# A blocked output projection with seven products in place of eight, behind an attention layer on one core

## The chip, the core and the metric

The kernel runs on one core of a Trainium2 chip. The metric is device time in microseconds of one execution. The core has a matrix engine (PE, with its weight loads as PEld), a vector engine (DVE), a scalar engine (ACT), a general engine (POOL) and a queue that issues transfers (SP); each runs its instructions in order and they wait for each other through semaphores.

## The reference

One post-norm layer over 1024 positions of width 1024. The input is normalised and modulated, one projection gives queries, keys, values and gates of 16 heads (8 forgetting heads, 8 stick-breaking heads of width 64), each head attends causally, the gated head outputs are concatenated to y, and the part that is changed here follows:

```python
y = jnp.concatenate([y_fox, y_sb], axis=-1) @ w_out[layer]
resid = DEEPNORM_ALPHA * x.astype(jnp.float32) + gate[:, None, :].astype(jnp.float32) * y.astype(jnp.float32)
x = _layer_norm(resid, ln_g[layer], ln_b[layer]).astype(dtype)
```

All is in float32. `w_out` is 1024 x 1024, `gate` is one row of 1024 numbers, the same for all positions.

## The kernel before

A product is computed from operands split in a high and a low part (`hi`, `lo`, type fp32r): three matmuls, high x high, low x high and high x low, take the place of one. The split costs a rounding copy for `hi` and a subtraction for `lo`.

The heads are handled in 8 pairs p = 0 to 7, of 128 rows each. A pair has 16 units (head h, query tile i of 128 positions), 128 units in all. A unit's scores come first, its transposition two units later (`LAG = 2`), and when both tiles of a 256-wide block are there `att_pv(p, h, j)` multiplies with v, and the 64 x 256 result is gated into `ty`. Between the units PE runs "fillers", generators that compute the in-projection of the pairs to come, one step per `yield`; a list of targets says how many steps run before each unit. The order of PE's instructions and the issue of the units is that of the Python code (`manual_schedule`); the other engines are ordered by a scheduler that follows the dependences. The last pair runs its tiles in falling order, so tiles 6 and 7 of y are finished first.

The output weights are prepared in the attention. `gen_split_out` (L812) runs beside the fillers of pairs 4 to 7: for each of 8 blocks of 128 rows and 2 halves of 512 columns, `fetch_w` loads a piece, POOL multiplies it by `gate` (L124), makes `hi` (L126) and `lo` (L127), and two transfers put them in `wo_dr` in memory; five filler steps lie between pieces (`SPACE = 5`). They come back by `load_wo` during the last fillers, into the buffers of the modulated input u, which is no longer needed then.

The outputs y of pairs 0 to 6 are stored to `y_dr` and loaded by tile with `load_y` (L832), where POOL makes `hi` and `lo` (L839, L840); y of pair 7 stays in SBUF (`y7h`, `y7l`, L520 to L525). The generator `tail` computes the output projection, some steps after each of the last units (`TAIL`) and the rest when the units are done, tile by tile in `OUT_ORDER = (6, 7, 4, 5, 2, 3, 0, 1)`. A step is `o_step(t, h, pr)`: three matmuls of 512 columns (L859 to L861). After 8 steps `o_half` adds ALPHA times x (L878, DVE) and takes the half's statistics on DVE (`bn_stats`, L879); after the second half come `bn_aggr` (L187), on POOL two steps on 128 x 1 (L189 adds epsilon, L190 takes the power -1/2), and on DVE two steps per half: L886 centres and multiplies by ln_g, L890 scales and adds ln_b; then the transfer out. The last tile's second half is cut in 320 and 192 columns, so that little is left after the last matmul.

Two accumulators in PSUM (`acc_tile`, a ring of two banks) serve the projection in turn: `o_6_0`, `o_6_1`, `o_7_0` and so on.

Of the kernel before, what the change touches and what calls it, by code (L numbers as in the profile page):

```python
# [27 lines left out]
def tile_hybrid_layer(  # L28
# [51 lines left out]
    SPACE = 5  # L80
# [29 lines left out]
    y_dr = dr.tile([NPAIR, P, SEQ], F32, tag="y_dr", name="y_dr")  # L110
    wo_dr = dr.tile([2, NPAIR, P, D], F32, tag="wo_dr", name="wo_dr")
# [256 lines left out]
    def gen_forget():  # L368
# [14 lines left out]
        for _ in range(FROW):  # L383
# [3 lines left out]
        nc.gpsimd.memset(tri, 1.0)  # L387
        nc.gpsimd.affine_select(out=tri, in_=tri, pattern=[[1, P]], base=0,
                                channel_multiplier=-1, compare_op=ALU.is_ge, fill=0.0)
# [43 lines left out]
    def att_scores(u, following):  # L433
# [28 lines left out]
        else:  # L462
# [14 lines left out]
            nc.gpsimd.tensor_tensor(be[:, :ke - 1], be[:, :ke - 1], kp[:, 1:ke], op=ALU.mult)  # L477
# [23 lines left out]
    y_last = []  # L501

    def att_pv(p, h, j):
# [298 lines left out]

    wo = {}

    def load_wo(pr):
        hi = big(f"u{pr}", 1, f"woh_{pr}", F32R)
        lo = big(f"v{pr}", 1, f"wol_{pr}", F32R)
        nc.sync.dma_start(hi.bitcast(F32), wo_dr[0, pr])
        nc.sync.dma_start(lo.bitcast(F32), wo_dr[1, pr])
        wo[pr] = (hi, lo)  # L810

    def gen_split_out():  # L812
        for pr in range(NPAIR):
            for h in range(2):
                s = slice(h * 512, h * 512 + 512)
                with after(*scaled[BEHIND:BEHIND + 1]):
                    hi, lo = fetch_w(f"o{pr}_{h}", w_out[pr * P:(pr + 1) * P, s], 512, gate[:, s])
                nc.sync.dma_start(wo_dr[0, pr, :, s], hi.bitcast(F32)[:, :512])
                nc.sync.dma_start(wo_dr[1, pr, :, s], lo.bitcast(F32)[:, :512])
                for _ in range(SPACE):  # L820
                    yield
# [8 lines left out]
    y_t = {}  # L830

    def load_y(t):  # L832
        ts_ = slice(t * P, (t + 1) * P)
        for p0, n in ((0, 4), (4, 3)):
            raw = raw_tile(f"yr_{t}_{p0}")[:, :n * P]
            nc.sync.dma_start(raw.rearrange("p (a q) -> p a q", q=P),
                              y_dr[p0:p0 + n, :, ts_].rearrange("a p q -> p a q"))
            hi, lo = y_t[t, p0 // 4] = ring_w(f"y_{t}_{p0}")
            nc.gpsimd.tensor_scalar(hi[:, :n * P], raw, 1.0, 1.0, op0=ALU.mult, op1=ALU.mult)  # L839
            nc.gpsimd.tensor_tensor(lo[:, :n * P], raw, hi.bitcast(F32)[:, :n * P], op=ALU.subtract)  # L840

    o_acc = {}
    OUT_ORDER = (6, 7, 4, 5, 2, 3, 0, 1)

    def groups(t):
        return ((0, 512), (512, 832), (832, 1024)) if t == OUT_ORDER[-1] else ((0, 512), (512, 1024))

    def o_step(t, h, pr):
        if pr == 0:
            o_acc[t, h] = (t_tile if h == 2 else acc_tile)(f"o_{t}_{h}")  # L850
        acc = o_acc[t, h]
        if pr == NPAIR - 1:
            yh, yl = (v[:, t * P:(t + 1) * P] for v in y_last)
        else:
            yh, yl = (v[:, pr % 4 * P:][:, :P] for v in y_t[t, pr // 4])
        hi, lo = wo[pr]
        s = slice(*groups(t)[h])
        acc = acc[:, :s.stop - s.start]
        nc.tensor.matmul(acc, yh, hi[:, s], start=(pr == 0), stop=False)  # L859
        nc.tensor.matmul(acc, yl, hi[:, s], start=False, stop=False)  # L860
        nc.tensor.matmul(acc, yh, lo[:, s], start=False, stop=(pr == NPAIR - 1))  # L861

    res = {}

    def o_half(t, h):
        ts_ = slice(t * P, (t + 1) * P)
        s = slice(*groups(t)[h])
        ng = len(groups(t))
        if h == 0:
            xr = big("k", 4, f"xr_{t}")  # L870
            nc.sync.dma_start(xr, x[ts_, :])
            res[t] = (att_tile(f"r_{t}"), xr, sb.tile([P, 3, 6], F32, tag="st", bufs=3, name=f"st_b{t}")[:, :ng, :])
        r, xr, st = res[t]
        last = t == OUT_ORDER[-1]

        acc = o_acc[t, h][:, :s.stop - s.start]
        to = acc if last else r[:, s]
        nc.vector.scalar_tensor_tensor(to, xr[:, s], ALPHA, acc, op0=ALU.mult, op1=ALU.add)  # L878
        nc.vector.bn_stats(st[:, h, :], to)  # L879
        if h == ng - 1:  # L880
            mv, rs = ln_finish(st, f"b{t}")
            cuts = [slice(*g) for g in groups(t)]
            mid = [o_acc[t, j][:, :c.stop - c.start] if last else r[:, c] for j, c in enumerate(cuts)]

            def first(j):
                nc.vector.scalar_tensor_tensor(mid[j], mid[j], mv[:, 0:1], lgb[0][:, 0, cuts[j]],  # L886
                                               op0=ALU.subtract, op1=ALU.mult)

            def second(j):
                nc.vector.scalar_tensor_tensor(r[:, cuts[j]], mid[j], rs[:, 0:1], lgb[0][:, 1, cuts[j]],  # L890
                                               op0=ALU.mult, op1=ALU.add)
                nc.sync.dma_start(out[ts_, cuts[j]], r[:, cuts[j]])

            if not last:
                for j in range(2):
                    first(j)
                    second(j)
                return
            for j in (1, 0, 2):
                first(j)  # L900
            c = cuts[1]
            nc.scalar.activation(r[:, c], mid[1], AF.Copy, scale=rs[:, 0:1])
            nc.gpsimd.tensor_tensor(r[:, c], r[:, c], lgb[0][:, 1, c], op=ALU.add)
            nc.sync.dma_start(out[ts_, c], r[:, c])
            for j in (0, 2):
                second(j)

    def gen_out_first(t):
        for h in range(2):
            for pr in range(NPAIR - 1):  # L910
                o_step(t, h, pr)
                yield

    def gen_out_last(t):
        for h in range(2):
            o_step(t, h, NPAIR - 1)
            o_half(t, h)
            yield

    def gen_out(t):  # L920
        for h in range(len(groups(t))):
            for pr in range(NPAIR):
                o_step(t, h, pr)
                if pr == NPAIR - 1:
                    o_half(t, h)
                yield


    def gen_last_g(p):
        tiles = fetch_m(p, 2)  # L930
        yield
# [64 lines left out]
    for k in range(len(units) + LAG + 1):  # L996
# [31 lines left out]
        if k == LAST:  # L1028
            load_y(6)
            load_ln()  # L1030
# [67 lines left out]
```

## Time and profile before

| | |
|---|---|
| median of 3 runs | 695.15 us (695.07 to 695.25) |
| the profiled execution | 695.03 us, span 693.3 us |
| granted clock of PE | 0.998 |
| busy: PE, DVE, POOL, ACT | 98%, 67%, 58%, 55% |
| transfers | 81.59 MB, mean 118 GB/s |

The page gives each engine's busy time as a share of the span, the chain of work that ended last, and groups of instructions; a group's row has the line, the engine, the operation, out <- in with shapes, the count, the busy time in us and the mean in ns of one, and then the idle time in front of them with what ended it. A row of the timeline has start and length in us. A row of stretches has, after the stretch and its length, busy us (and instruction count) of each engine, the granted clock, the DMA share and GB/s.

### The profile page before, as it was taken

Reading aid. Unit: us, or ns where it says so; the run is one execution under the profiler, and the core shown is the slowest. Engines: PE = TensorE matmul, PEld = TensorE weight load, DVE = VectorE, ACT = ScalarE, POOL = GpSimd, SP = SyncE. Lnnn points to the kernel's source line nnn. Section 1 sums busy time; section 2 is a strip of 40 time slices with the busy share of each in tenths; the row PEclk is TensorE's granted clock in tenths of the full one; section 3 lists DMA queues with packets and bytes.
Section 4 is the critical chain, followed back from the end, with each engine's and each line's share of the span. In section 5 each row is a group of like instructions: output and inputs, shape, how many; then the busy total and the mean of one; then the engine's idle time right before and its main releaser. Section 6 shows DMA issues by size and latency. Waiting matters only on the chain.

```text
span 693.3 us, 11762 instructions
## 1 busy us (share of the span) xinstructions
PE 678.1 (98%) x4031; PEld 592.2 (85%) x4031; DVE 465.9 (67%) x943; ACT 381.1 (55%) x857; POOL 399.1 (58%) x522
## 2 busy tenths in 40 slices
PE   8899999999999999999999999999999999999995
PEld 4689898888998888889998888889988889888885
DVE  6886868867658676767575665656665767774645
ACT  5566467756658666666674564655565666531000
POOL 5360086746438565556368787787685364655411
PEclk9999999999999999999999999999999999999999
DMA  9954531011102122112033554354352289143301
GB/s 328 415 205 160 168 104 47 25 40 45 47 9 69 41 54 54 38 47 61 23 116 126 161 151 139 114 171 149 115 160 73 62 289 355 56 161 116 119 34 61
DMA packets 44171, 81.59 MB, mean 118 GB/s; under 512 B 5136, under 2 KB 18768, under 8 KB 43344
## 3 DMA queue, kind: packets, MB, share of 16 engines
q1 hardware_dynamic: 42960, 76.65, 33.9%
q10 hardware_dynamic: 1152, 4.19, 1.9%
q8 instruction: 32, 0.52, 0.3%
q14 instruction: 27, 0.22, 0.1%
HBM read 60.34 MB, written 16.29 MB: 111 GB/s over the span
## 4 chain that ended last, share of the span: by engine, by line
PE 91%; DVE 4%; DMA 2%; ACT 2%; issue 0%; SPq 0%; DVEq 0%; ACTq 0%
PE pv L510 10%; PE m L285 10%; PE m L286 10%; PE m L287 10%; PE T L495 9%; PE S L446 5%; PE S L445 5%; PE o L861 4%; PE o L859 4%; PE o L860 4%; PE v L340 4%; PE v L342 4%; PE v L341 4%; DVE wss L228 1%; DMA wss<-in_w_ss_dram 1%; DMA x<-in_x_dram 1%
## 5 line engine op out<-in xcount | busy, mean ns | idle before, releaser
L285 PE MATMUL m<-uh,whi 128*128 128x512 f32 x304 | 126.3, 415 | 0.0
L286 PE MATMUL m<-ul,whi 128*128 128x512 f32 x304 | 119.8, 394 | 0.0
L287 PE MATMUL m<-uh,wlo 128*128 128x512 f32 x304 | 119.7, 394 | 0.0
L498 DVE TENSOR_TENSOR pt<-T,pt 128x512 fp32r<-128x512 f32 (+2 forms) x192 | 100.7, 551 | 17.4 <-ACT pt L497 16.1
L477 POOL TENSOR_TENSOR be<-be,kp 128x127 f32<-128x127 f32 (+3 forms) x64 | 78.0, 1218 | 37.5 <-DVE kp L475 27.5
L497 ACT CAST pt<-T 128x512 fp32r<-128x512 f32 (+2 forms) x192 | 85.8, 481 | 18.0 <-PE T L495 14.1
L471 DVE TENSOR_TENSOR_SCAN kp<-kp,floor 128x512 f32<-128x512 f32 (+2 forms) x64 | 65.1, 1017 | 34.1 <-ACT kp L465 32.6
L510 PEld LDWEIGHTS pv<-pt,v 128*128 128x128 f32 x640 | 83.3, 188 | 4.4 <-DVE pt L498 0.6
L510 PE MATMUL pv<-pt,v 128*128 128x256 f32 (+1 forms) x640 | 82.9, 275 | 0.3 <-DVE pt L498 0.3
L460 POOL TENSOR_SCALAR a<-a,l 128x1024 f32<-128x1024 f32 (+3 forms) x64 | 48.6, 759 | 48.5 <-DVE l L458 34.9
L287 PEld LDWEIGHTS m<-uh,wlo 128*128 128x128 f32 x304 | 57.1, 188 | 13.6
L457 ACT ACTIVATE a<-a,nm 128x1024 f32<-128x1024 f32 (+3 forms) x64 | 49.9, 780 | 34.1 <-DVE nm L452 33.7
L445 PE MATMUL S<-k,q 128*128 128x512 f32 (+5 forms) x192 | 67.0, 350 | 0.9 <-ACT be L466 0.7
L446 PE MATMUL S<-kl,qz 128*128 128x512 f32 (+5 forms) x192 | 65.5, 342 | 0.0
L285 PEld LDWEIGHTS m<-uh,whi 128*128 128x128 f32 x304 | 57.3, 189 | 8.8 <-DVE kl L273 0.4
L286 PEld LDWEIGHTS m<-ul,whi 128*128 128x128 f32 x304 | 57.4, 189 | 7.9
L452 DVE CUSTOM_DVE_ANT_0 a<-S,fb 128x1024 f32<-128x1024 f32 (+3 forms) x64 | 48.4, 756 | 21.4 <-PE S L446 9.9
L519 POOL TENSOR_TENSOR ty<-ty,sg 64x256 f32<-64x256 f32 x64 | 47.2, 738 | 25.6 <-DVE ty L518 12.5
L465 ACT ACTIVATE kp<-S 128x128 f32<-128x128 f32 (+3 forms) x64 | 41.8, 653 | 34.5 <-PE S L446 31.1
L340 PE MATMUL v<-whi_v,uh 128*128 128x256 f32 (+1 forms) x192 | 56.1, 292 | 0.7 <-DVE kl L273 0.7
L419 ACT CAST qz<-q 64x128 fp32r<-64x128 f32 x128 | 37.4, 297 | 34.0 <-PE S L446 32.8
L342 PE MATMUL v<-wlo_v,uh 128*128 128x256 f32 (+1 forms) x192 | 54.1, 282 | 0.0
(291 smaller groups left out, 1592.5 us busy)
## 6 DMA issues: line engine op xcount, KB each, us to landing
raw<-in_w_qkg_dram SPq DMA_DIRECT2D x38, 256.0 KB, 2.8
wss<-in_w_ss_dram SPq DMA_DIRECT2D x6, 1024.0 KB, 7.6
x<-in_x_dram SPq DMA_DIRECT2D x8, 512.0 KB, 7.0
k<-k SPq DMA_DIRECT2D x32, 128.0 KB, 2.4
wg<-in_w_gate_dram SPq DMA_DIRECT2D x8, 512.0 KB, 4.5
raw_o<-in_w_out_dram SPq DMA_DIRECT2D x16, 256.0 KB, 3.1
fb<-f_dr ACTq DMA_DIRECT2D x8, 512.0 KB, 4.1
wo_dr<-whi_o SPq DMA_DIRECT2D x16, 256.0 KB, 2.0
```

What stands on the lines that cost most here:

```text
L285: nc.tensor.matmul(acc, hi[:, c], u_hi[kt][:, s], start=(kt == 0), stop=False)
L286: nc.tensor.matmul(acc, hi[:, c], u_lo[kt][:, s], start=False, stop=False)
L287: nc.tensor.matmul(acc, lo[:, c], u_hi[kt][:, s], start=False, stop=(kt == NB - 1))
L340: nc.tensor.matmul(acc[:, :n], u_hi[kt][:, ts_], hi[:, s], start=(kt == 0), stop=False)
L342: nc.tensor.matmul(acc[:, :n], u_hi[kt][:, ts_], lo[:, s], start=False, stop=(kt == NB - 1))
L445: nc.tensor.matmul(S[:, s, :w], qst[p][h][:, qs], kst[p][h][:, ks], start=True, stop=False)
L446: nc.tensor.matmul(S[:, s, :w], z, klo[p][:, ks], start=False, stop=True)
L471: last_dve = nc.vector.tensor_tensor_scan(rv, rv, floor[:, :ke - lo], initial=0.0, op0=ALU.mult, op1=ALU.max)
L477: nc.gpsimd.tensor_tensor(be[:, :ke - 1], be[:, :ke - 1], kp[:, 1:ke], op=ALU.mult)
L497: nc.scalar.copy(hi[:, :n, qo:qo + P], t3)
L498: lows[:] = [nc.vector.tensor_tensor(lo[:, :n, qo:qo + P], t3, hi.bitcast(F32)[:, :n, qo:qo + P], op=ALU.subtract)]
L510: nc.tensor.matmul(acc[:, q0:256], vt[p][:, kb, h * P:(h + 1) * P], pt[:, kb % 4, q0:], start=(part == 0 and kb == 0), stop=(part == 1 and ...
```

## The change

The projection of a pair of tiles, (t, t2), is treated as a product of 2 x 2 blocks. With a1, a2 the halves of y of tile t along the 1024 summed numbers, b1, b2 those of t2, and W11, W12, W21, W22 the four 512 x 512 blocks of the gated weights, these sums are made:

```
S1 = b1 + b2    S2 = S1 - a1    S3 = a1 - b1    S4 = a2 - S2
T1 = W12 - W11  T2 = W22 - T1   T3 = W22 - W12  T4 = T2 - W21
```

and seven block products: a1 W11, S3 T3, S2 T2, a2 W21, S1 T1, b2 T4, S4 W22. The four output blocks are sums of these. A product is 4 blocks of 128 rows x 3 terms, 12 matmuls of 512 columns; before, a tile had 48 of them.

`gen_early` runs a1 W11 and S3 T3 of all pairs of tiles: they need y of the head pairs 0 to 3 alone. Their sums go to `res`, which holds ALPHA x to begin with (L940). `gen_late` runs the other five for one pair of tiles after another, in an accumulator V (`ov`) that is read after each of S2 T2, S1 T1 and S4 W22 and goes on summing, and in a second one (`ow`) for b2 T4 and a2 W21. Each of these five ends in an add on DVE (L948). The weights' sums are made by DVE, the copies `hi` now by ACT, and 28 pieces of `hi` and `lo` instead of 16 go to `wo_dr`, spread over the fillers from pair 2 on by `SPACE` and `EACH`. Weight blocks T1 and T4 are loaded into the buffers of W11 and T3 when all early products are done, W22 into buffers of the attention.

All of y goes through `y_dr`, now laid out by tile. `late_y` makes S1, S2 and S4 on POOL (L909, L910, L918), `put_y` a high part on ACT and a low part on POOL (L883).

`normalise` takes, for all tiles but the last two, the mean and the mean square by two passes of ACT over the whole row (`mean_square`), then the two 128 x 1 steps on POOL (L980, L981), then as before two steps per half on DVE (L961, L967). The last two tiles keep `bn_stats`, and the last one its cut in 512, 320 and 192. The mask `tri` of the forget gates is made by one DVE instruction instead of two on POOL.

```diff
-    SPACE = 5
+    SPACE = (7, 38, 0, 24, 0)
+    EACH = (5, 3, 3, 2)
...
-        if p == NPAIR - 1:
-            if not y_last:
-                y_last.extend([big("sg", 2, "y7h", F32R), big("kl", 2, "y7l", F32R)])
-            yh, yl = y_last
-            nc.scalar.copy(yh[r, qs], yt[r, :])
-            nc.gpsimd.tensor_tensor(yl[r, qs], yt[r, :], yh.bitcast(F32)[r, qs], op=ALU.subtract)
-        else:
-            nc.sync.dma_start(y_dr[p, r, qs], yt[r, :])
+        nc.sync.dma_start(y_dr[2 * j:2 * j + 2, r, p * P:p * P + P].rearrange("t r c -> r t c"),
+                          yt[r, :].rearrange("r (t c) -> r t c", t=2))
...
+    W11, T3, T2, W21, T1, T4, W22 = range(7)
...
     def gen_split_out():
...
+        def put(b, j, w):
+            hi, lo = ring_w(f"o{b}_{j}")
+            nc.scalar.copy(hi[:, :512], w)
+            with after(*scaled[BEHIND:BEHIND + 1]):
+                nc.gpsimd.tensor_tensor(lo[:, :512], w, hi.bitcast(F32)[:, :512], op=ALU.subtract)
+            s = slice(j % 2 * 512, j % 2 * 512 + 512)
+            nc.sync.dma_start(wo_dr[b, j // 2, 0, :, s], hi.bitcast(F32)[:, :512])
+            nc.sync.dma_start(wo_dr[b, j // 2, 1, :, s], lo.bitcast(F32)[:, :512])
...
+            scaled_by(r11, gs[0])
+            scaled_by(r12, gs[1])
+            put(W11, j, r11)
+            yield from wait(EACH[j])
+            less(r11, r12, r11)
+            put(T1, j, r11)
...
+    def put_y(x_, key, w):
+        hi, lo = y_op[x_, key] = ring_w(f"y{key}_{x_[0]}")
+        nc.scalar.copy(hi[:, :512], w)
+        nc.gpsimd.tensor_tensor(lo[:, :512], w, hi.bitcast(F32)[:, :512], op=ALU.subtract)
...
+    def late_y(x_):
...
+        a1, a2, b1, b2 = a[:, :512], a[:, 512:], b[:, :512], b[:, 512:]
+        nc.gpsimd.tensor_tensor(b1, b1, b2, op=ALU.add)
+        nc.gpsimd.tensor_tensor(a1, b1, a1, op=ALU.subtract)
+        put_y(x_, "s2", a1)
+        sides = [("22", b2), ("12", a2)]
+        if x_ == PAIRS[0]:
+            sides.reverse()
+        put_y(x_, *sides[0])
+        put_y(x_, "s1", b1)
+        put_y(x_, *sides[1])
+        nc.gpsimd.tensor_tensor(a2, a2, a1, op=ALU.subtract)
+        put_y(x_, "s4", a2)
...
+    def add_to(t, a, b, acc, op=ALU.add):
+        r = res[t][:, a:b]
+        nc.vector.tensor_tensor(r, r, acc[:, :b - a], op=op)
...
+    def mean_square(t):
...
+        nc.scalar.activation(spare, r, AF.Copy, accum_out=mv[:, 0:1])
+        nc.scalar.activation(mv[:, 0:1], mv[:, 0:1], AF.Copy, scale=-1.0 / D)
+        nc.scalar.activation(spare, r, AF.Square, bias=mv[:, 0:1], accum_out=rs[:, 0:1])
+        nc.gpsimd.tensor_scalar(rs[:, 0:1], rs[:, 0:1], 1.0 / D, EPS, op0=ALU.mult, op1=ALU.add)
+        nc.gpsimd.tensor_tensor(rs[:, 0:1], rs[:, 0:1], mhalf, op=ALU.pow)
...
+    tail = chain([gen_early(PAIRS[:2]), gen_early(PAIRS[2:])] + [gen_late(x_) for x_ in PAIRS])
```

Three places show how the queues change. First PE, in the middle of the projection. Before, the start of tile 0 (`o_0_0` is its first half's accumulator, `woh`/`wol` the weights' parts by head pair, `whi_y`/`wlo_y` those of y):

```order
L859 MATMUL o_0_0_7946<-woh_0_6802,whi_y_0_0_7799 128x512
L860 MATMUL o_0_0_7946<-woh_0_6802,wlo_y_0_0_7800 128x512
L861 MATMUL o_0_0_7946<-wol_0_6803,whi_y_0_0_7799 128x512
L859 MATMUL o_0_0_7946<-woh_1_6818,whi_y_0_0_7799 128x512
L860 MATMUL o_0_0_7946<-woh_1_6818,wlo_y_0_0_7800 128x512
L861 MATMUL o_0_0_7946<-wol_1_6819,whi_y_0_0_7799 128x512
```

After, the end of S2 T2 of tiles 2 and 3 (`ov_2` is V) and the start of b2 T4 in the other accumulator, `ow_3`:

```order
L928 MATMUL ov_2_7999<-woh_2_1_7056,whi_ys2_2_7841 128x512
L928 MATMUL ov_2_7999<-woh_2_1_7056,wlo_ys2_2_7842 128x512
L928 MATMUL ov_2_7999<-wol_2_1_7057,whi_ys2_2_7841 128x512
L928 MATMUL ow_3_8013<-woh_5_0_7665,whi_y22_2_7845 128x512
L928 MATMUL ow_3_8013<-woh_5_0_7665,wlo_y22_2_7846 128x512
L928 MATMUL ow_3_8013<-wol_5_0_7666,whi_y22_2_7845 128x512
```

An accumulator was left after 24 matmuls; now after 12, and the next product takes the other one. A weight block serves one product, where it served one step.

Second DVE, at the normalisation of tile 5 and the adds after it. Before (`r_5` is the row of tile 5, `mv_b5` its statistics, `rs_b5` the factor from POOL, `r_2` the next tile):

```order
L878 SCALAR_TENSOR_TENSOR r_5_7731<-xr_5_7729,o_5_1_7735 128x512
L879 BN_STATS st_b5_7732<-r_5_7731 128x6
L187 BN_AGGR mv_b5_7773<-st_b5_7732 128x2
L886 SCALAR_TENSOR_TENSOR r_5_7731<-r_5_7731,mv_b5_7773,lngb_6879 128x512 x2
L890 SCALAR_TENSOR_TENSOR r_5_7731<-r_5_7731,rs_b5_7775,lngb_6879 128x512 x2
L878 SCALAR_TENSOR_TENSOR r_2_7835<-xr_2_7833,o_2_0_7784 128x512
L879 BN_STATS st_b2_7836<-r_2_7835 128x6
L878 SCALAR_TENSOR_TENSOR r_2_7835<-xr_2_7833,o_2_1_7839 128x512
```

After (`res_1_0`, `res_1_1` and `res_v` are the rows of tiles 4, 5 and of 2 and 3):

```order
L948 TENSOR_TENSOR res_1_1_6995<-res_1_1_6995,ov_4_7866 128x512
L948 TENSOR_TENSOR res_1_0_6994<-res_1_0_6994,ow_4_7931 128x512
L961 SCALAR_TENSOR_TENSOR res_1_1_6995<-res_1_1_6995,mv_b5_7917,lngb_6933 128x512 x2
L967 SCALAR_TENSOR_TENSOR res_1_1_6995<-res_1_1_6995,rs_b5_7918,lngb_6933 128x512 x2
L948 TENSOR_TENSOR res_1_0_6994<-res_1_0_6994,ov_4_7866 128x512
L948 TENSOR_TENSOR res_v_7073<-res_v_7073,ov_2_7999 128x512
L961 SCALAR_TENSOR_TENSOR res_1_0_6994<-res_1_0_6994,mv_b4_7985,lngb_6933 128x512 x2
L948 TENSOR_TENSOR res_v_7073<-res_v_7073,ow_3_8013 128x512
L967 SCALAR_TENSOR_TENSOR res_1_0_6994<-res_1_0_6994,rs_b4_7986,lngb_6933 128x512 x2
```

Before, the steps of tile 5 stood between the adds of two tiles of 48 matmuls each; now the scaling of tile 5, which needs `rs_b5`, stands ahead of the add from `ov_4`, and the scaling of tile 4 ahead of the third add from the pair after.

Third POOL, where those factors are made. Before, in the same part of the program (`ty` is the attention's output, `rs_b4` tile 4's factor):

```order
L839 TENSOR_SCALAR whi_y_3_0_7703<-yr_3_0_7701 128x512
L525 TENSOR_TENSOR y7l_7059<-ty_7_0_0_7650,y7h_7058 64x256
L840 TENSOR_TENSOR wlo_y_3_0_7704<-yr_3_0_7701,whi_y_3_0_7703 128x512
L189 TENSOR_SCALAR rs_b4_7679<-mv_b4_7677 128x1
L190 TENSOR_TENSOR rs_b4_7679<-rs_b4_7679,mhalf_89 128x1
L839 TENSOR_SCALAR whi_y_3_4_7709<-yr_3_4_7707 128x384
L840 TENSOR_TENSOR wlo_y_3_4_7710<-yr_3_4_7707,whi_y_3_4_7709 128x384
```

After (`yr2`, `yr3` are y of tiles 2 and 3, `wlo_...` the low parts):

```order
L910 TENSOR_TENSOR yr2_7835<-yr3_7836,yr2_7835 128x512
L981 TENSOR_TENSOR rs_b6_7822<-rs_b6_7822,mhalf_89 128x1
L883 TENSOR_TENSOR wlo_ys2_2_7842<-yr2_7835,whi_ys2_2_7841 128x512
L883 TENSOR_TENSOR wlo_y22_2_7846<-yr3_7836,whi_y22_2_7845 128x512
L518 TENSOR_TENSOR ty_7_1_0_7899<-ty_7_1_0_7899,sg_7_6859 64x256
L883 TENSOR_TENSOR wlo_ys1_2_7850<-yr3_7836,whi_ys1_2_7849 128x512
L980 TENSOR_SCALAR rs_b5_7918<-rs_b5_7918 128x1
L981 TENSOR_TENSOR rs_b5_7918<-rs_b5_7918,mhalf_89 128x1
L883 TENSOR_TENSOR wlo_y12_2_7854<-yr2_7835,whi_y12_2_7853 128x512
L918 TENSOR_TENSOR yr2_7835<-yr2_7835 128x512
```

The `hi` steps have left POOL, the sums have come, and between the factors `rs_b6` and `rs_b5` stand three low parts and one piece of the attention.

More of the change, by code (lines that the diff above doesn't have):

```diff
@@ L842, in tile_hybrid_layer @@
[L842 to L853, printed above, removed]
-        else:
[L855 to L861, printed above, removed]
@@ L863, in tile_hybrid_layer @@
-    res = {}
-    def o_half(t, h):
-        ts_ = slice(t * P, (t + 1) * P)
[L867 to L926, printed above, removed]
+    PAIRS = ((6, 7), (4, 5), (2, 3), (0, 1))
```

241 lines of the change are left out of this document (197 added, 44 removed).

## The prediction

> **What bounds the kernel now.** I read the page first: busy shares, then the chain that ended last.
>
> ```profile
> span 693.3 us, 11762 instructions
> PE 678.1 (98%) x4031; PEld 592.2 (85%) x4031; DVE 465.9 (67%) x943; ACT 381.1 (55%) x857; POOL 399.1 (58%) x522
> PE 91%; DVE 4%; DMA 2%; ACT 2%; issue 0%; SPq 0%; DVEq 0%; ACTq 0%
> ```
>
> The matrix engine is busy for 98% of the span and holds 91% of the chain. The waits of PE say whether anything ever holds it in the middle:
>
> ```profile
> engine line waited for: us in total, times, longest us
> PE st_q L591 <- ACT uh L248: 3.5, 4, 1.4
> ...
> PE pv L510 <- DVE pt L498: 0.3, 1, 0.3
> PE S L445 <- DVE nm L452: 0.2, 1, 0.2
> ```
>
> The largest waits belong to the start; the attention's cost fractions of a microsecond. The busy times by stretch show how much room the other engines have:
>
> ```profile
> core 0: us, PE busy (x) PEld busy (x) DVE busy (x) ACT busy (x) POOL busy (x), PEclk, DMA share, GB/s
> 220.00:360.00 140.00, 140.00 (x881) 125.56 (x880) 98.19 (x158) 91.43 (x202) 82.39 (x114) 1.00 0.21 58
> 360.00:560.00 200.00, 199.74 (x1225) 177.08 (x1224) 124.94 (x330) 114.17 (x282) 144.20 (x165) 1.00 0.41 127
> 628.00:686.00 58.00, 58.00 (x275) 48.08 (x273) 31.03 (x49) 1.45 (x4) 20.73 (x26) 1.00 0.24 83
> ```
>
> In all three PE has no gap. From 360 to 560 us, where the output weights are split, POOL is the fullest helper (72%); in the last 58 us, output projection alone, DVE stands at 53% and POOL at 36%. So a matmul taken out should be worth its whole duration, as long as the helpers can go on feeding a PE that works faster. The question is the last stretch, where the change puts new work on POOL and ACT.
>
> **The change part by part. Matmuls.** The last tile shows the cost by width, since it runs 24 matmuls of 512 columns, then 24 of 320, then 24 of 192:
>
> ```profile
> 676.39 0.39 PE L859 MATMUL o<-woh,whi_y 128*128 128x512 f32 x1
> ...
> 679.87 0.31 PE L859 MATMUL o<-woh,whi_y 128*128 128x320 f32 x1
> ...
> 683.38 0.25 PE L859 MATMUL o<-woh,whi_y 128*128 128x192 f32 x1
> ...
> 685.92 0.28 PE L861 MATMUL o<-wol,y7h 128*128 128x192 f32 x1
> ```
>
> A record's length overlaps its neighbours, so I take distances between starts. Between the first two rows lie 15 matmuls of 512: 3.48 / 15 = 0.232 us. The 24 of 320 take 3.51 us, 0.146 each; 23 of 192 take 2.54 us, 0.110 each. Before, the projection has 360 + 24 + 24 = 408 matmuls. After, each of four pairs of tiles has 7 products of 4 blocks x 3 terms = 12 matmuls; in the last pair three products are cut in 320 + 192: 300 of 512, 36 of 320, 36 of 192, 372 in all. Saved: 60 x 0.232 - 12 x (0.146 + 0.110) = 13.92 - 3.07 = **10.85 us** of PE. The shortened program says this exactly; it is no guess.
>
> **Weight blocks during the attention.** The prices of the split, before and after:
>
> ```profile
> L127 POOL TENSOR_TENSOR wlo_o<-raw_o,whi_o 128x512 fp32r<-128x512 f32 x16 | 20.8, 1298 | 0.4
> L124 POOL TENSOR_TENSOR raw_o<-raw_o,gate 128x512 f32<-128x512 f32 x16 | 20.8, 1297 | 3.4 <-DMA raw_o<-in_w_out_dram 3.4
> L126 POOL TENSOR_SCALAR whi_o<-raw_o 128x512 fp32r<-128x512 f32 x16 | 10.0, 622 | 0.6
> L578 ACT CAST hw<-raws 128x512 fp32r<-128x512 f32 x5 | 2.9, 621 | 0.0
> L498 DVE TENSOR_TENSOR pt<-T,pt 128x512 fp32r<-128x512 f32 x96 | 64.7, 687 | 16.2 <-ACT pt L497 15.5
> ```
>
> POOL goes from 20.8 + 20.8 + 10.0 = 51.6 us to 44 x 1.30 = 57.2 us, but spread from about 220 us on instead of from 360 us, so its fullest stretch gets emptier. ACT gets 28 x 0.62 = 17.4 us, DVE 16 x 0.69 = 11.0 us (a two-input op of 512 from the nearest row; its operands lie in SBUF, where L498 has one in PSUM). Against about 340 us with ACT at 60% and DVE at 66%, each has over 100 us free. What covers them is the two units by which the attention's score stage runs ahead of its product with v. The queues are in order: behind a 1.30 us subtraction waits POOL's scaling of probabilities, behind a copy the ACT evictions that PE waits for. Bounds: nothing (every copy falls in the lag) to 5 us (a fifth of the 28.4 us added to ACT and DVE reaches PE). I take **+0.3**, the size of the waits shown, since the lag has so far absorbed nearly all of the 1,250 helper instructions of these two stretches.
>
> **Transfers.** The weight blocks are 7 x 2 MB instead of 8 MB, and three of the seven are loaded during the projection, because they take over buffers of blocks already used.
>
> ```profile
> GB/s 219 300 416 264 238 401 377 396 411 414 424 405 413 422 394 386 412 426 414 430 391 408 426 422 410 417 295 73 13 0 0 0 0 0 0 0 16 0 9 187
> woh<-wo_dr SPq DMA_DIRECT2D x8, 512.0 KB, 8.5
> ```
>
> The first row is 560 to 600 us, where the weights come in: about 410 GB/s. The first two early products that free buffers end some 7 us before the late products start (call that moment T); T1, T4 and W22 with the y of two tiles are 7 MB or 17 us at that rate, so W22 is there at T + 10, or 11 to 12 with x and other pieces between; its halves are needed at about T + 12 and T + 13.4 (five products of 2.78 us end at 13.9). That fits by about 1 us; at 300 GB/s, the second-lowest reading while weights move, the 7 MB take 23 us and the block is 3 us late. I take zero and keep 0 to 3.
>
> The y of the last head pair goes through memory instead of staying in SBUF, and all y in pieces half as long. One write and one read take some 5 us by these rows:
>
> ```profile
> y_dr<-ty SPq DMA_DIRECT2D x56, 64.0 KB, 1.9
> yr<-y_dr SPq DMA_DIRECT2D x8, 256.0 KB, 3.5
> ```
>
> For tiles 6 and 7 attention ends about two units before T, and early products stand between: the operand is there at about T + 0, no slack and no wait; the other tiles have 14 us and more. I count nothing.
>
> **The projection's helpers.** The rows for the new tail:
>
> ```profile
> L840 POOL TENSOR_TENSOR wlo_y<-yr,whi_y 128x512 fp32r<-128x512 f32 x8 | 10.4, 1297 | 0.6
> L519 POOL TENSOR_TENSOR ty<-ty,sg 64x256 f32<-64x256 f32 x64 | 47.2, 738 | 25.6 <-DVE ty L518 12.5 <-issue 8.0 <-PE T L495 1.7
> L457 ACT ACTIVATE a<-a,nm 128x1024 f32<-128x1024 f32 x8 | 9.2, 1154 | 6.7 <-DVE nm L452 6.7
> L457 ACT ACTIVATION_READ_ACCUMULATOR a<-a,nm 128x1 f32 x64 | 12.0, 188 | 0.0
> L878 DVE SCALAR_TENSOR_TENSOR r<-xr,o 128x512 f32<-128x512 f32 x14 | 9.5, 686 | 20.3 <-PE o L861 20.2
> L890 DVE SCALAR_TENSOR_TENSOR r<-r,rs_b,lngb 128x512 f32<-128x512 f32 x14 | 10.1, 748 | 3.4 <-POOL rs_b L190 3.4
> ```
>
> and, from the timeline, the two tiny steps that turn a variance into a factor:
>
> ```profile
> 653.99 0.77 POOL L189 TENSOR_SCALAR rs_b<-mv_b 128x1 f32<-128x1 f32 x1 [0.38 <-DVE mv_b L187]
> 654.85 0.93 POOL L190 TENSOR_TENSOR rs_b<-rs_b,mhalf 128x1 f32<-128x1 f32 x1
> ```
>
> One pair's five late products are 60 x 0.232 = 13.9 us of PE. In that time POOL has 3 sums and 5 subtractions of 1.30, two pairs of tiny steps of 0.77 + 0.93 and, while the attention lasts, a 0.74: 10.4 + 3.4 + 0.7 = 14.5 us. So POOL, at 36% before, is as full as PE, and 0.6 us per pair over it. DVE has 5 adds of 0.69 and 8 steps of 0.75: 9.5 us, which fits.
>
> The wait that this makes: DVE's queue is in order, and the add that empties an accumulator stands behind the two scaling steps of the tile before, which wait for POOL's power. Count from p, the end of a tile pair's T1 product: add 0.69, two passes on ACT with their reads and the small copy 2 x (1.15 + 0.19) + 0.19 = 2.87, POOL 0.77 + 0.93 = 1.70, two scalings 1.50, the next add 0.69. With five hand-overs at about 0.06 that is p + 7.75. PE needs this accumulator's slot (there are two) three products later, at p + 8.35. Slack: **0.6 us**, if POOL is idle when the sum of squares comes. But POOL is nearly always in a 1.30 op, and what stands ahead of the tiny steps in its order is such an op: about one op late, 1.3 - 0.6 = 0.7 us of PE each, for six tiles (all but the last pair, which keeps the old statistics) 4.2 us. POOL's own excess of 0.6 carries over from the first pair to the second and on to the third, 2 periods or 1.2 us, but of that half sits in waits already counted; I take 0.6. Together **+4.8 us**. Bounds: 0 (operands prepared early enough, all slack used) and 10 (each of the six waits behind two ops and meets the copies on ACT too).
>
> The end keeps its form (split last half, same steps from 685.92 on), so nothing is saved or added there.
>
> **The sum.** On the profiled execution of 695.03 us (span 693.3, 1.7 around it): 695.03 - 10.85 + 4.8 + 0.3 = 689.3. The median shown is 695.15, 0.1 above the profiled one, so I say **689.4 us**.
>
> **The rivals.** About 0.2% (1.4 us) is what a measurement of this kernel can tell from no change.
>
> A, the forecast: 689.4, by 687 to 692. 48%.
>
> B, everything is saved: POOL's chain stays within the slack because the subtractions run ahead. 695.15 - 10.85 = 684.3. For it: PE had no gap in the old tail at all. Against: 14.5 us of POOL beside 13.9. 18%.
>
> C, slower: DVE and POOL hinder each other where both read SBUF, in the normalisation. The row of before that bears on it:
>
> ```profile
> 642.01 1.30 POOL L840 TENSOR_TENSOR wlo_y<-yr,whi_y 128x512 fp32r<-128x512 f32 x1
> ...
> 642.76 1.76 DVE L886 SCALAR_TENSOR_TENSOR r<-r,mv_b,lngb 128x512 f32<-128x512 f32 x2
> ```
>
> and all 14 of its kind (shortest, median, longest in ns):
>
> ```profile
> L886 DVE SCALAR_TENSOR_TENSOR r<-r,mv_b,lngb x14: 739/748/1099, 604.9 to 676.9; 128x512 f32<-128x512 f32 x14
> ```
>
> Two steps that take 2 x 0.75 alone took 1.76 beside a POOL subtraction: 0.35 us lost in one of 14, the POOL op at its usual 1.30. If instead each of a pair's 8 such steps held up POOL for half its length, POOL would have 8 x 0.375 = 3.0 us more, 17.5 against 13.9: 3.6 us per pair, 10.8 over three, on top of A's 4.8 and 0.3: 700.2. It ends slower once the losses pass 10.85 us, that is with over 1.9 us more per pair than A has. 10%. The Trainium skill, page "SBUF — State Buffer", section "Who interferes with whom", has the rule for this: a DVE instruction with two SBUF inputs and a GpSimd instruction that reads SBUF want the same port pair, whoever comes first holds it for its whole length and the other "fully blocks". Of that the trace agrees with one stretch of 0.35 us, where the whole rest of the POOL op, 642.76 to 643.31, is 0.55; by that rule the time is C's.
>
> D, the late blocks come late: 2 us more than A, 691.4. 12%.
>
> E, the attention pays: 5 us instead of 0.3, 694.1, by 3 on either side. 12%, of which 5 parts are faster by over 0.2%, 6 within it and 1 slower.
>
> That the change doesn't do what it says is excluded by the count, 408 to 372.
>
> **Numbers.** Faster by over 0.2%: A, B, D and 5 parts of E, 0.83; same: 6 parts of E, 0.06; slower: C and 1 part of E, 0.11. The range takes A, B, D and most of E: 684.3 to 694.5; C and the rest of E, some 15%, are left out. A's own range is 687 to 692.
>
> **What would show it.** In the profile of the changed kernel: projection matmuls at 0.232 us; PE's waits with new rows in the last 60 us, on DVE's add (the accumulator's slot), each 0.3 to 1.3 us, sum 3 to 7; POOL over 90% busy between the first late product and the last pair; DVE's scaling steps idle for the power of POOL, ending right before such a gap. Wrong if PE has no gaps there (B), if the waits are on DMA of the weight blocks (D), if gaps lie between 220 and 560 us (E), or if the L967 and L961 steps last over 1 us in the mean (C). A time under 684 or over 695.5 refutes the sum.

## The result, and the profile after

The changed kernel takes 715.35 us (median of 4 runs, 713.95 to 716.34) against 695.2 us (median of 4) before: a ratio of 1.0285, 95% interval 1.0272 to 1.0297. It is slower by 20.2 us, where 689.4 us was forecast. The profiled execution took 716.34 us, span 714.5. The kernel before was run again beside each set of experiments below, with medians of 695.46 to 695.75 us. From the page:

```profile
span 714.5 us, 11957 instructions
PE 678.4 (95%) x3995; PEld 589.2 (82%) x3995; DVE 502.2 (70%) x962; ACT 423.3 (59%) x937; POOL 434.7 (61%) x522
PE 71%; DVE 11%; ACT 5%; POOL 5%; DMA 3%; issue 3%; SPq 0%; POOLq 0%; ACTq 0%; DVEq 0%
```

PE runs 36 instructions fewer and is busy as long as before (678.1): its matmuls got slower somewhere by about the 10.85 us that were saved (most of it through the clock, see below), and 21 us of idle time came on top. PE holds 71% of the chain, where it held 91%. Its waits:

```profile
engine line waited for: us in total, times, longest us
PE S L445 <- DVE nm L452: 4.3, 3, 2.7
PE T L496 <- DVE pt L499: 4.0, 2, 3.8
...
PE m L287 <- DVE kl L275: 3.2, 1, 3.2
PE ow L928 <- DVE res L948: 2.9, 1, 2.9
PE ov L928 <- DVE res L948: 1.9, 2, 1.3
```

Three new rows belong to the attention, where there was nothing over a microsecond, and the last two rows shown to the projection. Where the time goes can be dated, since PE's order up to the projection is the same in both kernels. The in-projection has 304 matmuls of high x high form; the n-th of them in one timeline against the n-th in the other gives how late PE is. Numbers 88 and 92, counted from 0, before and after:

```profile
255.76 0.39 PE L285 MATMUL m<-uh,whi 128*128 128x512 f32 x1
...
259.77 0.39 PE L285 MATMUL m<-uh,whi 128*128 128x512 f32 x1
```

```profile
256.34 0.39 PE L287 MATMUL m<-uh,whi 128*128 128x512 f32 x1
...
265.94 0.40 PE L287 MATMUL m<-uh,whi 128*128 128x512 f32 x1
```

Between two neighbours 4 us apart the lateness goes from 0.58 to 6.17 us. The whole list has only a few such jumps:

| place in the changed kernel, us | late before | late behind | lost |
|---|---|---|---|
| 256 to 266 | 0.58 | 6.17 | 5.6 |
| 279 to 285 | 6.20 | 6.77 | 0.6 |
| 451 to 507 | 6.85 | 8.62 | 1.8 |
| 540 to 554 | 8.63 | 12.47 | 3.8 |
| 569 to 581 | 12.47 | 18.44 | 6.0 |
| projection and end (21.2 at the end, 10.85 saved) | 18.50 | 21.2 + 10.85 | 13.5 |

So 18 us are lost in the attention and 13.5 in the projection, against 10.85 saved. Three causes show in the timeline.

**First, a DVE step with both inputs in SBUF.** The rows at the first jump:

```profile
252.75 0.61 POOL L128 TENSOR_SCALAR whi<-raw 128x512 fp32r<-128x512 f32 x1
...
253.34 7.29 DVE L829 TENSOR_TENSOR wo_raw<-wo_raw 128x512 f32<-128x512 f32 x1
253.36 1.99 POOL L477 TENSOR_TENSOR be<-be,kp 128x1023 f32<-128x1023 f32 x1
...
255.32 1.29 POOL L823 TENSOR_TENSOR wlo_o<-wo_raw,whi_o 128x512 fp32r<-128x512 f32 x1
...
256.57 1.29 POOL L817 TENSOR_TENSOR wo_raw<-wo_raw,gate 128x512 f32<-128x512 f32 x1
...
258.82 1.25 POOL L129 TENSOR_TENSOR wlo<-raw,whi 128x512 fp32r<-128x512 f32 x1
...
260.55 0.41 DVE L517 TENSOR_TENSOR ty<-pv,ty 64x256 f32<-64x256 f32 x1
...
261.70 1.61 PE L496 MATMUL T<-ident,be 128*128 128x128 f32 x8 [3.81 <-DVE pt L499]
```

L829 is the sum of two weight blocks. It starts at 253.34 and ends at 260.6, half a microsecond after POOL's unbroken row of steps ends at 260.07. POOL's steps have their usual length (L477 with 1023 columns takes 2.00 us in the mean of before). Behind L829 in DVE's queue stand the steps of the attention, and PE's two units of lead are used up: a gap of 3.81 us. All 16 sums:

```profile
L829 DVE TENSOR_TENSOR wo_raw<-wo_raw x16: 693/1316/7290, 239.0 to 556.4; 128x512 f32<-128x512 f32 x16
```

They were taken at 0.69 us each; the longest, 7.29, 5.51 and 3.72 us, stand right ahead of jumps. Those three ended only when POOL paused. Seven of the 16 got in between two POOL steps, and then the POOL step behind was the longer one:

```profile
244.80 1.30 POOL L823 TENSOR_TENSOR wlo_o<-wo_raw,whi_o 128x512 fp32r<-128x512 f32 x1
...
245.71 0.94 DVE L829 TENSOR_TENSOR wo_raw<-wo_raw 128x512 f32<-128x512 f32 x1
246.05 3.01 POOL L129 TENSOR_TENSOR wlo<-raw,whi 128x512 fp32r<-128x512 f32 x2
```

Here L829 takes 0.94 us, and the two L129 steps 3.01 in place of 2.6. What decides whether DVE gets in is not shown.

**Second, PE's clock.** Up to the last matmul the granted clock (column PEclk) is either full or half, and it changes only on a grid of 3.41 us: the halves begin at 262.06, 572.68 and 675.08 us, 91 and 30 such steps apart. The windows of this grid around the gaps of PE of 3.81, 2.72, 3.18 and 2.90 us:

```profile
core 0: us, PE busy (x) PEld busy (x) DVE busy (x) ACT busy (x) POOL busy (x), PEclk, DMA share, GB/s
258.65:262.06 3.41, 0.36 (x4) 0.39 (x4) 3.41 (x5) 0.62 (x1) 2.18 (x4) 1.00 0.22 79
262.06:265.48 3.42, 3.42 (x13) 2.93 (x12) 3.13 (x5) 1.66 (x3) 1.89 (x2) 0.50 0.39 120
541.96:545.37 3.41, 1.69 (x9) 1.08 (x7) 3.41 (x2) 0.11 (x1) 2.66 (x3) 1.00 0.45 141
545.37:548.78 3.41, 2.41 (x11) 1.86 (x11) 2.16 (x7) 3.19 (x7) 0.88 (x1) 1.00 0.48 151
569.27:572.68 3.41, 1.00 (x6) 0.52 (x4) 0.45 (x3) 1.70 (x4) 1.05 (x1) 1.00 0.67 225
572.68:579.50 6.82, 6.05 (x16) 4.79 (x17) 2.45 (x5) 2.73 (x7) 4.26 (x6) 0.50 0.85 275
671.67:675.08 3.41, 1.14 (x5) 0.57 (x4) 3.41 (x3) 0.62 (x1) 3.33 (x3) 1.00 0.81 324
675.08:681.90 6.82, 6.19 (x15) 4.92 (x16) 3.21 (x6) 3.83 (x7) 6.21 (x6) 0.50 0.10 38
```

Where PE worked for only 0.36, 1.00 and 1.14 us of a window, the clock is half in what follows, for 3.41, 6.82 and 6.82 us, and PE loses some 2 to 3 us more. The gap of 2.72 us was divided between two windows with 1.69 and 2.41 us of work, and the clock stayed. So the gap's length alone does not decide: in the kernel with the early high parts on POOL (below) the same gap of 2.72 us fell into one window, and the clock halved:

```profile
543.13:546.54 3.41, 0.69 (x4) 0.40 (x3) 3.23 (x4) 1.35 (x3) 1.25 (x2) 1.00 0.09 34
546.54:549.96 3.42, 3.42 (x11) 2.69 (x10) 2.32 (x6) 3.30 (x9) 2.31 (x2) 0.50 0.60 197
```

In all traces of this case, as far as the clock is recorded and up to the last matmul, every such window with under 1.6 us of PE's work was followed by half the clock, and none with over 1.71 us was. The Trainium skill, page "TensorE: Matmul & The Clock Gate", part 1, says that an idle window of about 3.4 us halves the clock and as long a busy one brings it back; here windows in which PE still worked for up to 1.6 us were enough.

**Third, a late load at the head of ACT's queue.** The jump at 569 us:

```profile
562.01 0.54 SPq L874 DMA_DIRECT2D lngb<-in_ln_g_dram  x1
562.61 0.47 SPq L875 DMA_DIRECT2D lngb<-in_ln_b_dram  x1
563.17 0.89 SPq L896 DMA_DIRECT2D ye<-y_dr  x2
...
570.95 0.62 ACT L882 CAST whi_y<-ye 128x512 fp32r<-128x512 f32 x1 [2.72 <-issue]
...
573.45 0.80 PE L287 MATMUL m<-uh,whi 128*128 128x512 f32 x1 [3.18 <-DVE kl L275]
```

The first early y is issued at 563.17, behind the loads of ln_g and ln_b, and its high part starts at 570.95. For the 2.72 us before that ACT stands still, though the attention's evictions are queued behind that copy. The 6.0 us lost here are PE's gap of 3.18 us and 2.8 us at the lower clock.

**In the projection** DVE's scaling steps meet POOL's subtractions and sums:

```profile
671.46 1.29 POOL L883 TENSOR_TENSOR wlo_y<-yr,whi_y 128x512 fp32r<-128x512 f32 x1
...
671.52 3.44 DVE L967 SCALAR_TENSOR_TENSOR res<-res,rs_b,lngb 128x512 f32<-128x512 f32 x2 [0.44 <-POOL rs_b L981]
...
672.83 1.59 POOL L918 TENSOR_TENSOR yr<-yr 128x512 f32<-128x512 f32 x1
674.38 1.72 POOL L909 TENSOR_TENSOR yr<-yr 128x512 f32<-128x512 f32 x1
...
674.89 0.68 DVE L948 TENSOR_TENSOR res<-res,ov 128x512 f32<-128x512 f32 x1
...
675.71 0.77 PE L928 MATMUL ow<-woh,whi_y 128*128 128x512 f32 x1 [2.90 <-DVE res L948]
```

Two steps of 0.75 us take 3.44 together, POOL's steps go from 1.30 to 1.6 and 1.7, the add that frees the accumulator stands behind, and PE waits 2.90 us. Such gaps are 0.63, 1.31, 2.90 and 0.90 us (5.7); the product behind the longest takes 5.26 us and the next 3.22 in place of 2.78 (2.9 for the clock); two waits in the last units of the attention take 1.5; and the end after the last matmul is 8.4 us long in place of 7.1. That is 11.4 of the 13.5 us; the rest was not followed.

### The profile page after: what moved, and what is told of

The parts are those of the page before. It is cut to its first block, busy times and chain, and to the rows that moved or that the text cites. A ratio compares the mean times of both kernels' runs of the same rounds, so it can differ in the third digit from the quotient of the medians.

```text
span 714.5 us, 11957 instructions
## 1 busy us (share of the span) xinstructions
PE 678.4 (95%) x3995; PEld 589.2 (82%) x3995; DVE 502.2 (70%) x962; ACT 423.3 (59%) x937; POOL 434.7 (61%) x522
## 4 chain that ended last, share of the span: by engine, by line
PE 71%; DVE 11%; ACT 5%; POOL 5%; DMA 3%; issue 3%; SPq 0%; POOLq 0%; ACTq 0%; DVEq 0%
PE pv L509 9%; PE m L287 8%; PE m L288 8%; PE m L289 8%; PE T L496 8%; PE S L445 4%; PE S L446 4%; PE v L342 3%; PE v L344 3%; PE v L343 3%; DVE wo_raw L829 3%; PE oe L928 3%; PE ow L928 1%; DVE wss L230 1%; DMA wss<-in_w_ss_dram 1%
## 5 line engine op out<-in xcount | busy, mean ns | idle before, releaser
L499 DVE TENSOR_TENSOR pt<-T,pt 128x512 fp32r<-128x512 f32 (+2 forms) x192 | 100.8, 551 | 19.2 <-ACT pt L498 17.8
L477 POOL TENSOR_TENSOR be<-be,kp 128x127 f32<-128x127 f32 (+3 forms) x64 | 77.8, 1217 | 36.4 <-DVE kp L475 24.6
```

The costliest lines, as they stand in the source:

```text
L477: scaled[:] = [*scaled[-3:], nc.gpsimd.tensor_tensor(be[:, :ke - 1], be[:, :ke - 1], kp[:, 1:ke], op=ALU.mult)]
L499: lows[:] = [nc.vector.tensor_tensor(lo[:, :n, qo:qo + P], t3, hi.bitcast(F32)[:, :n, qo:qo + P], op=ALU.subtract)]
```

## The experiments

**The sums on POOL**, undoing the place of the new DVE work:

```diff
         def less(to, x_, y_):
-            nc.vector.tensor_tensor(to, x_, y_, op=ALU.subtract)
+            with after(*scaled[BEHIND:BEHIND + 1]):
+                nc.gpsimd.tensor_tensor(to, x_, y_, op=ALU.subtract)
```

> The changed kernel with the 16 sums of weight blocks (L829) on POOL instead of DVE. Theory 1 (a DVE step with both inputs in SBUF is held up by POOL's stream; one of them lasted 7.29 us in place of 0.69, and PE fell behind by 5.6, 0.6, 1.3, 0.4 and 3.9 us right after five such steps): these 11.8 us come back, about 703.5 us, with DVE's other steps at their old length. Rival (the attention is disturbed because ACT, DVE and POOL simply have more queued): POOL gets 16 x 1.30 = 20.8 us more, so nothing comes back or it gets worse, 715 to 718.

Measured: 699.76 us (698.45 to 702.49), 15.6 less than the changed kernel. Of the jumps of the list only 0.5 and 0.4 us are left ahead of the early y: PE is 0.57 us late, relative to before, after number 240 and 2.1 at number 303. POOL runs the 16 sums in 20.7 us and this cost nothing that shows. That it gives more than 11.8 comes from the early y: the same copies on ACT lose 1.2 us here in place of 6.0.

**The early high parts on POOL**, as before the change:

```diff
-        nc.scalar.copy(hi[:, :512], w)
+        if key in ("11", "s3"):
+            nc.gpsimd.tensor_scalar(hi[:, :512], w, 1.0, 1.0, op0=ALU.mult, op1=ALU.mult)
+        else:
+            nc.scalar.copy(hi[:, :512], w)
```

> The changed kernel with the high parts of the early y (eight copies, keys 11 and s3) on POOL, as all of them were before, instead of ACT. Theory 2 (the copy stands at the head of ACT's queue until its load lands, 7.8 us after its issue, and behind it stand the evictions that PE waits for): the 6.0 us lost between 569 and 581 us come back, about 709.3. Rival (the late load holds up whichever queue takes the copy): POOL's scaling stands behind it instead, PE loses the same 6, about 715.

Measured: 709.44 us, 5.9 less. The lateness goes from 12.5 to 12.8 between number 288 and 303, so the jump of 6.0 us is down to 0.3. The load is as late as it was; POOL waits for it now, and nobody waits for POOL:

```profile
570.93 0.62 POOL L883 TENSOR_SCALAR whi_y<-ye 128x512 fp32r<-128x512 f32 x1 [4.62 <-DMA ye<-y_dr]
```

**Both edits:**

> Both edits together. If the two losses are independent, 11.8 + 6.0 come back: 697.5, and what is left, 697.5 - (695.2 - 10.85) = 13.2 us, is lost in the projection itself. If one of them only uncovers the other, 703 to 709.

Measured: 701.94 us (700.92 to 702.42), not less but 2.2 more than with the sums on POOL alone, whose runs reach up to 702.49, so the two are not told apart. At number 303 PE is late by 2.6 us in this kernel and by 2.1 in the other: with the sums gone from DVE there is no 6 us to win at the early y. The spans of the two profiled executions, 699.9 and 696.6 us, differ mostly by the clock: the longest gap is 2.87 us in both, but half the clock follows for 6.83 us here and for 3.41 us there, and a gap of 1.84 us in the attention's last units brings another 3.41 us. That is 5.9 us more of PE's work at half the clock, an estimated 2.9 us.

**One input in place of two.** DVE's queue is left as it is, and the operand is taken away:

```diff
-            nc.vector.tensor_tensor(to, x_, y_, op=ALU.subtract)
+            nc.vector.bn_stats(to[:, :6], x_)
```

> The changed kernel with each of the 16 sums (L829) replaced on DVE by a bn_stats of one of its two operands, 512 columns, which takes 0.69 us as well but has one input in SBUF; the weights' sums are left out. DVE's queue, its waits and all other engines' work stay as they are. Theory 1: every one of them lasts about 0.69 us and 11.8 us come back, about 703.5. Rival (a step more in DVE's queue at these places costs this, whatever it reads): 715.

Measured: 701.57 us, 13.8 less, and all 16 steps have the length that was expected of the sums:

```profile
L829 DVE BATCH_NORM_STATS2 wo_raw<-wo_raw x16: 667/689/696, 238.9 to 544.4; 128x6 f32<-128x512 f32 x16
```

Same places in the queue, same 512 columns read, one SBUF input fewer: the loss is not the longer queue's. This step also writes 6 columns in place of 512, but that is not what decides: L499, with one input in PSUM and 512 columns written, takes 0.69 us in the mean of its 96 steps in the changed kernel, and with the addend in PSUM below, 512 columns written too, the steps have their own length.

**Another form of the same sum** (`scalar_tensor_tensor`, x times 1.0 minus y):

> The changed kernel with the 16 sums on DVE as scalar_tensor_tensor (x times 1.0, minus y) instead of tensor_tensor: the same two inputs in SBUF, the same order. In the projection steps of this form lasted up to 1.8 us beside a POOL subtraction that took 1.7, whereas L829's tensor_tensor lasted up to 7.29 beside POOL steps of their usual 1.29. If the form decides how the two share: at most about 1.8 us each, and most of the 11.8 us come back, 704 to 707. If it is the density of POOL's steps at these places: 714 to 716 as before.

Measured: 709.67 us (706.17 to 712.72), between the two expectations, and the steps are as they were, to some nanoseconds:

```profile
L829 DVE SCALAR_TENSOR_TENSOR wo_raw<-wo_raw x16: 692/1312/7291, 238.7 to 556.1; 128x512 f32<-128x512 f32 x16
```

So the form decides nothing about the steps' length. That the density of POOL's steps does is not shown: at 279.04, 446.44 and 534.51 us a sum got in after one step of an unbroken row, at 253.34 only after the whole row. What this kernel gains lies elsewhere: in its profiled execution, the slowest of the four (span 710.9), PE is late by 16.0 us at number 303 in place of 18.5, nearly all of it made at the early y. Why the other three runs are faster still isn't known.

The four runs on the projection start from the kernel with the sums on POOL (699.8), which still has its gaps. **An addend in PSUM** (`spares[t]` is the throw-away output of the squares):

```diff
-                nc.vector.scalar_tensor_tensor(r[:, s], r[:, s], rs[:, 0:1], lgb[0][:, 1, s],
+                nc.vector.scalar_tensor_tensor(r[:, s], r[:, s], rs[:, 0:1], spares[t][:, s],
```

> The kernel with the sums on POOL (699.8), and in the projection each scaling step of the six tiles that take the mean square (L968) adds a tile in PSUM in place of ln_b in SBUF, so that one input in SBUF is left; ln_b is left out for these tiles and something else added. The wait for POOL's factor stays. There the projection loses 6.3 us in four gaps of PE (0.7, 1.35, 2.9, 1.4) and 1.9 at a lower clock after the longest. Theory 3 (the loss is the same hindrance: the two steps took 2.48 and 3.44 us in place of 1.50, and POOL's subtractions 1.7 in place of 1.3): the steps take 1.5 again, the gap of 2.9 falls below 1.5, about 695. Rival (the chain over ACT's two passes and POOL's factor is simply too long for the place where the steps stand in DVE's queue): 698.5 to 700.

Measured: 693.31 us (692.04 to 694.84), 6.5 less. The steps (the 8 of 12 whose rows are called `res`) and POOL's subtractions are at their own length, and PE's waits on DVE's adds are 1.5 us in all:

```profile
L968 DVE SCALAR_TENSOR_TENSOR res<-res,rs_b,spare x8: 734/744/749, 640.2 to 662.7; 128x512 f32<-128x512 f32 x8
```

```profile
L884 POOL TENSOR_TENSOR wlo_ys<-yr,whi_ys 128x512 fp32r<-128x512 f32 x12 | 15.6, 1302 | 1.1 <-ACT whi_ys L883 1.0
```

**Shorter statistics, another place, no factor:**

```diff
-            mv, rs = mean_square(t)
-            centre = ALU.add
+            st = sb.tile([P, 3, 6], F32, tag="st", bufs=3, name=f"st_c{t}")
+            for h in range(2):
+                nc.vector.bn_stats(st[:, h, :], r[:, h * 512:h * 512 + 512])
+            mv, rs = ln_finish(st[:, :2, :], f"b{t}")
+            centre = ALU.subtract
```

> The kernel with the sums on POOL (699.8), with the statistics of all tiles by bn_stats and bn_aggr on DVE, as before the change, instead of two passes on ACT. The chain from the last add to POOL's factor gets shorter by about 2.9 - 0.9 = 2.0 us, while DVE has 1.6 us more per tile. If the chain's length is the cause of the gaps: about 695. If the hindrance between DVE and POOL is: 699 to 702, since the scaling steps fall on the same subtractions.

```diff
+            with after(ins):
+                nc.vector.scalar_tensor_tensor(r[:, s], r[:, s], rs[:, 0:1], lgb[0][:, 1, s],
+                                               op0=ALU.mult, op1=ALU.add)
```

> The kernel with the sums on POOL (699.8), with the scaling steps of each tile queued on DVE behind the add that PE needs next, instead of ahead of it (tile 5's behind the add of S4 W22, tile 4's behind the next pair's add of b2 T4, and so on). No step is made shorter. If the gaps come from the add standing behind the wait for POOL's factor, whatever makes that late: 6.3 + 1.9 us less a rest of about 2, 693 to 694, below the kernel before the change. If DVE as a whole has too much to do (hindered steps counted): 699.

```diff
-                nc.vector.scalar_tensor_tensor(r[:, s], r[:, s], rs[:, 0:1], lgb[0][:, 1, s],
+                nc.vector.scalar_tensor_tensor(r[:, s], r[:, s], mv[:, 0:1], lgb[0][:, 1, s],
```

> The kernel with the sums on POOL (699.8), with the scaling steps of the six tiles taking the mean as their factor instead of POOL's power, so they wait for no POOL step (which still runs); these rows are not normalised then. Both inputs stay in SBUF. If the wait for the factor makes the gaps: 693 to 694. If the hindrance does: 698 to 700, and the steps last well over 0.75 us each.

Measured: 697.01, 697.31 and 697.34 us. Each is worth 2.4 to 2.8 us, between the two expectations; none comes near the 6.5 of the operand's place. The runs of the kernel that they start from spread over 4 us, so the three can't be ranked. The scaling steps of the second and third of these kernels (behind the next add; without the factor) are still long:

```profile
L959 DVE SCALAR_TENSOR_TENSOR res<-res,rs_b,lngb x8: 752/1778/1812, 639.8 to 665.2; 128x512 f32<-128x512 f32 x8
```

```profile
L968 DVE SCALAR_TENSOR_TENSOR res<-res,mv_b,lngb x8: 740/1459/1790, 638.8 to 665.4; 128x512 f32<-128x512 f32 x8
```

Even with no factor to wait for, they take 1.46 us in the median in place of 0.74. So the order in DVE's queue and the chain have a part, the hindrance the larger one.

**A version that keeps the whole computation.** ln_b is copied once to the PSUM banks of the scores, which are free by then:

```diff
-        spare = s_tile(f"spare_{t}").rearrange("p a b -> p (a b)")
+        if not lnb:
+            lnb.append(s_tile("lnb").rearrange("p a b -> p (a b)"))
+            nc.scalar.copy(lnb[0], lgb[0][:, 1, :])
+        spare = att_tile(f"spare_{t}")
...
-                nc.vector.scalar_tensor_tensor(r[:, s], r[:, s], rs[:, 0:1], lgb[0][:, 1, s],
+                nc.vector.scalar_tensor_tensor(r[:, s], r[:, s], rs[:, 0:1], lnb[0][:, s],
```

> The kernel with the sums on POOL, and ln_b copied to PSUM (the bank pair of the scores) when the attention is done; the six scaling steps add it from there, and the squares' throw-away output goes to SBUF instead. All of the computation is done. Theory 3: as with the other addend in PSUM, the steps take 0.74 us each and POOL's subtractions 1.30; one copy of 1.1 us on ACT is new: about 694. If the gain of that run came from leaving out ln_b or from anything else than the place of the operand: 698 to 700.

Measured: 694.69 us, ratio to before 0.9988 (0.9979 to 0.9997): 5.1 of the 6.5 us are kept. With the scaling steps deferred as well:

> The last kernel with the scaling steps queued behind the add that PE needs next as well. Alone, that was worth 2.5 us (697.3 against 699.8), with a step of 1.77 us in the way; with steps of 0.74 us, what is left of PE's waits on DVE's adds is 1.5 us: 692 to 693, below the kernel before by 2 to 3.

Measured: 694.09 us (692.87 to 697.78), less gain than expected and a wide spread. In the profiled execution (span 693.6) no wait on DVE's adds is left among the larger ones, but transfers are late again at the early y. This time PE waits for the keys:

```profile
PE S L445 <- DMA k<-k: 2.2, 1, 2.2
```

So the last edit moves the ln loads away from there:

```diff
-        if k == LAST:
+        if k == LAST + 8:
             load_ln()
```

> The last kernel with the two loads of ln_g and ln_b (1 MB) issued eight units later, so that they don't stand ahead of the first early y. Theory 2 (the high part of the early y waits on ACT for its load): what the kernels with the sums on POOL still lose at that place, 1.2 us, goes: 691 to 692. Rival (the weight blocks' loads hold it up, not these): no change.

Measured: 691.8 us (691.67 to 692.39), ratio to before 0.995 (0.9935 to 0.9965): 3.8 us faster than the kernel before and 23.6 than the change as it was. The spread is gone too. PE's longest wait beyond the start is now one that the last kernel had as well:

```profile
span 690.0 us, 11961 instructions
```

```profile
PE ow L929 <- ACT whi_y L883: 2.0, 1, 2.0
```

PE is 1.6 us late at number 303, so its projection loses 690.0 - 693.3 + 10.85 - 1.6 = 5.9 us, where the changed kernel's loses 13.5.

## Why the prediction was wrong, step by step

The profiled execution is 27 us longer than the forecast for it: some 11.5 us in the attention, 6.0 at the early y, 8.7 in the projection and 0.6 ahead of the first jump.

**Matmuls: right.** 372 matmuls at 0.232 us; a product that waits for nothing takes 2.79 us (forecast 2.78).

**Weight blocks during the attention: the step that failed.** It said that 16 sums on DVE take 0.69 us each, with the price from a step that has one input in PSUM, and said so in passing. The sums have both in SBUF and, beside POOL's stream, took 31.8 us in all, where the same steps with one input took 11.0; PE lost 11.8 us. The bound of 5 us was no bound: it took a share of the added work as the most that can be lost, while one step of 0.69 us alone cost 5.6. What it named as the risk, an ACT queue made longer, was not it: with 28 copies and the same queue the loss goes when the second input goes.

**The rule was there, and used in the wrong place.** Rival C had this hindrance, with the row of 1.76 us and the Trainium skill's page "SBUF — State Buffer", section "Who interferes with whom", but only for the normalisation. The same section names a two-input step with both operands in SBUF; L829 was one, beside a row of POOL steps without a gap. The trace agrees that DVE is blocked, but not that the first to come goes first: L829 began at 253.34, while POOL's L128 was still running, and six more POOL steps on SBUF that began later, from L477 at 253.36 on, went ahead of it. For the projection C forecast 10.8 us of it; the runs put it at 6.5, the clock behind the longest gap included.

**Transfers: half right.** The weight blocks came in time, as forecast: PE has no wait on them. (The bound went by 300 GB/s as the second-lowest reading of its row, but 238 and 264 stand there too.) What came late was the y of the early products, which the sum left out: it counted y as having no cost since it looked at the late products only. In the changed kernel that cost 6.0 us, through ACT's queue and a clock at half.

**The projection's helpers: the mechanism right, the size off.** The add behind the scaling step behind POOL's factor was the wait of PE, at four of the six tiles, with gaps of 0.6 to 2.9 us. They sum to 5.7 us, near the 4.8 forecast, but that nearness is luck: the forecast took 1.50 us for two scaling steps and found its loss in a POOL step in the way, while the two steps took 2.45 to 3.47 us at five of these tiles. With the addend in PSUM, where they take 1.5 us, the waits on these adds come to 1.5 us only. The other 7.8 of the 13.5 us were not in the sum: 2.9 for the clock, 1.5 of waits in the attention's last units, 1.3 at the end, which it took as unchanged, and 2.1 that were not followed. Without the hindrance and with the steps in a better place 5.9 us are left.

**The clock: not in the forecast at all.** It priced a gap at its length. Three gaps of 2.9 us and more cost another 1.8 to 2.9 us each.

**The range** took rival C's ends out as one in ten. A loss in the attention (E) and the hindrance (C) came together, from one cause; the chances had taken them as exclusive. The signs of both are in the profile: gaps of PE between 220 and 560 us, and scaling steps (L967) of 1.35 us in the mean, with L961 at 0.79.

## What to carry to other kernels

Before work moves to DVE beside a busy POOL, count how many of its inputs lie in SBUF: a price from a step with one input in PSUM says nothing for one with two, and the cost can be as long as POOL's unbroken row, not as the step. Move such a step to POOL, or put a constant operand in PSUM. A copy that waits for a load belongs in a queue that PE doesn't wait for; and a gap of PE of 2 to 3 us can cost twice its length.

## What the hardware showed that was not expected

- A DVE step with two SBUF inputs can lose to POOL's whole row of steps: 7.29 us in place of 0.69, over 6.7 us of POOL steps that were not slowed themselves. In other places it gets in between two POOL steps and both suffer: 0.94 us for 0.69 and 3.01 for 2.6 at 245.71 us, and in the projection up to 1.78 us for 0.74 on DVE and 1.7 for 1.30 on POOL. What decides which of the two happens was not settled; the form of the instruction doesn't (7.29 in both forms).
- PE's clock fell to half for 3.4 or 6.8 us after a window of 3.41 us in which PE worked for less than about half, so where a gap falls on that grid counts beside its length: a gap of 1.84 us was followed by half the clock, one of 2.72 us in one trace was and in another was not.
